# The gate softmax of a product-key layer moved out of its top-k, behind blocks of the expert product

## The chip, the cores and the metric

One core of one Trainium2 chip runs the whole program. The metric is device time in microseconds (us) of one execution; smaller is better. Engines are named as in the profile: PE is TensorE, ACT is ScalarE, DVE is VectorE, POOL is GpSimd, SP is SyncE, which issues most of the DMAs.

## The reference

A decoder block on 512 tokens of width 1024: a gated convolution and a differential attention, a layer norm, then a PEER channel mixer and another layer norm. The change lies in the mixer, which has 16,384 experts (rows of `u` and `v`), 8 heads and 16 chosen experts for each token and head:

```python
q = (xc @ wq).reshape(PEER_CHUNK, PEER_HEADS, 2, PEER_DHALF)
sc = jnp.einsum('chpd,hpnd->chpn', q, keys)
s1, i1 = lax.top_k(sc[:, :, 0], PEER_TOPK)
s2, i2 = lax.top_k(sc[:, :, 1], PEER_TOPK)
cand = (s1[..., :, None] + s2[..., None, :]).reshape(...)
top_s, pos = lax.top_k(cand, PEER_TOPK)
eidx = jnp.take_along_axis(cidx, pos, axis=-1)
g = jax.nn.softmax(top_s, axis=-1)
act = jax.nn.gelu(jnp.einsum('chkd,cd->chk', u[eidx], xc))
return jnp.einsum('chk,chkd->cd', g * act, v[eidx])
```

The softmax `g` over the 16 best scores of a token and head is what the change moves.

## The kernel before, in words

The tokens form four chunks of 128. For chunks 0 to 2 (384 tokens) the mixer is computed densely: for each of 128 blocks of 128 experts, `dense_u` (L426) forms u·x for all 384 tokens on TensorE (24 matmuls of 128x384, three per slice of the contraction, because float32 is split in a high and a low part) and applies Gelu on ScalarE (L432). A dense matrix of gates, zero for experts that a token has not chosen, is multiplied in later (L561), and `dense_v` forms the second product with `v`. Chunk 3 gathers its experts' rows by DMA (`gather_steps`, L495).

The weights of a block come by DMA; `split` (L71) makes the high part on ScalarE (`whi`, L72) and the low part (`wlo`, L73) on GpSimd for blocks 0 to 13 (`NPOOL`) and on VectorE from block 14 on. Two PSUM tiles (`psH`) take the products, so block j+2 can start only when block j's Gelu has read its tile. 42 blocks of u·x (`HS_BUFS`) precede the second product; from there the two products alternate until the end.

The gate matrix is made meanwhile. `topk` (L276) runs on VectorE for one chunk after the other: `top16` (L268) finds the 16 largest scores of each half and head by pairs of MAX8, FIND_INDEX8 and MATCH_REPLACE8, then those of the candidates `cand`; L299 to L304 make the softmax (subtract, Exp on ScalarE, sum, reciprocal, product `g`); L305 to L330 turn positions into the expert's two index halves `idf`. `topk_transpose` (L333) transposes `idf` and `g` on TensorE (L337, L338), and ScalarE and VectorE copy them out as `iT` and `gT` (L340 to L343). From those, the loop at L455 makes one-hot tiles `oa`, `bh` and `bl` for 16 tokens at a time on VectorE (L462 to L465), multiplies them on TensorE (L470, L471), copies the result out on ScalarE (`stg`, L472) and writes it to a buffer `G_D` in device memory (L473). There are 24 such steps. `dense_w` (L544) reads `G_D` back (`gt`, L553) before the second product starts, and loads rows of v (`vr`, L540).

Each engine executes its instructions in one fixed order, which a scheduler computes when the program is built, from its own model of the durations. The source steers it only by edges: `tc.issue_after(x)` keeps what is made inside it behind instruction x on the same engine. The table TK says behind which expert block each chunk's transposes are put; the code around it, before:

```python
    for c in range(NDC):
        for j in range(*TK[c]):
            mm = dense_u(j)
        with tc.issue_after(mm.ins):
            topk_transpose(c, *picked[c])
```

With `TK = ((0, 3), (3, 10), (10, 14))` chunk 0's transposes stand behind block 2, chunk 1's behind block 9, chunk 2's behind block 13.

Of the kernel before, what the change touches and what calls it, by code (L numbers as in the profile page):

```python
# [9 lines left out]
F32 = mybir.dt.float32  # L10
# [4 lines left out]
AF = mybir.ActivationFunctionType  # L15
ALU = mybir.AluOpType
AX = mybir.AxisListType
# [7 lines left out]
PH = 8  # L25
# [3 lines left out]
ND = 384  # L29
# [11 lines left out]
VR = 3  # L41
WB = 4
GA = 4
TK = ((0, 3), (3, 10), (10, 14))
GI2 = 8
GP = 3
GSCALE = 16384.0
# [6 lines left out]
def build(nc, tc, I, out, dbg=None):  # L54
# [155 lines left out]
    for h in range(NH):  # L210
        ps = proj(12 + h)
        nc.scalar.copy(out=qz[0:64, h, 0, :], in_=ps[0:64])
        nc.scalar.copy(out=qz[64:128, h, 1, :], in_=ps[64:128])
        ps = proj(16 + h)
        nc.scalar.copy(out=kT[:, h, :], in_=ps)
        ps = proj(20 + h)
# [42 lines left out]
    tk = tk_ctx.enter_context(load_pool("topk", bufs=1, side="left"))  # L259
# [16 lines left out]
    def topk(tk, sc, nb):  # L276
        m = tk.tile([128, 2, PH, 16], F32, name="m", bufs=nb)
        ix = tk.tile([128, 2, PH, 16], U32, name="ix")
        for h in range(PH):
# [10 lines left out]
            cand[:, :, 64:112].rearrange("p h (a b) -> p h a b", b=4),  # L290
            m[:, 0, :, 4:16].unsqueeze(3).broadcast_to([128, PH, 12, 4]),
            m[:, 1, :, 0:4].unsqueeze(2).broadcast_to([128, PH, 12, 4]), op=ALU.add)
        tsc = tk.tile([128, PH, 16], F32, name="tsc")
        pos = tk.tile([128, PH, 16], U32, name="pos")
        for h in range(PH):
            top16(tk, tsc[:, h, :], pos[:, h, :], cand[:, h, :], 112)
        g = tk.tile([128, 16, PH], F32, name="g", bufs=nb)
        gx = tk.tile([128, PH, 16], F32, name="gx")
        nc.vector.tensor_tensor(gx, tsc, tsc[:, :, 0:1].broadcast_to([128, PH, 16]), op=ALU.subtract)  # L299
        nc.scalar.activation(gx, gx, AF.Exp)  # L300
        gs = tk.tile([128, PH], F32, name="gs")
        nc.vector.tensor_reduce(gs, gx, axis=AX.X, op=ALU.add)
        nc.vector.reciprocal(gs, gs)
        nc.vector.tensor_tensor(g.rearrange("p k h -> p h k"), gx, gs.unsqueeze(2).broadcast_to([128, PH, 16]), op=ALU.mult)  # L304
        u1 = tk.tile([128, PH, 16], U32, name="u1")  # L305
        u2 = tk.tile([128, PH, 16], U32, name="u2")
        ab = tk.tile([128, 2, 16, PH], F16, name="ab")
# [10 lines left out]
        idf = tk.tile([128, 2, 128], F32, name="idf", bufs=nb)  # L318
# [9 lines left out]
        for n in (8, 4, 2):  # L328
            nc.vector.tensor_tensor(e[:, :, 0:n], e[:, :, 0:n], e[:, :, n:2 * n], op=ALU.add)  # L329
        nc.vector.tensor_tensor(idf, e[:, :, 0], e[:, :, 1], op=ALU.add)  # L330
        return idf, g

    def topk_transpose(c, idf, g):  # L333
        cs = slice(c * 128, (c + 1) * 128)
        tp = psG.tile([128, 4, 128], F32, name="psX", bufs=1)
        for p in range(2):
            nc.tensor.transpose(tp[:, p, :], idf[:, p], ident)  # L337
        nc.tensor.transpose(tp[:, 2, :], g.rearrange("p k h -> p (k h)"), ident)  # L338
        for e in range(2):
            nc.scalar.copy(out=iT[:, :, cs, e], in_=tp[:, 0:2, :])  # L340
            nc.scalar.activation(gT[:, 0, cs, e], tp[:, 2, :], AF.Copy, scale=GSCALE)
        for e in range(2):
            nc.vector.scalar_tensor_tensor(gT[:, 1, cs, e], tp[:, 2, :], GSCALE, gT[:, 0, cs, e],  # L343
                                           op0=ALU.mult, op1=ALU.subtract)
# [81 lines left out]
    def dense_u(j):  # L426
        uh, ul = wblock(I["uT"][j], nc.gpsimd if j < NPOOL else nc.vector)
        ps = psH.tile([128, S], F32, name="psH")
        for k in range(NK):
            mm = mm3(ps[:, 0:ND], uh[:, k, :], ul[:, k, :], x1h[:, k, 0:ND], x1l[:, k, 0:ND], k == 0, k == NK - 1)  # L430
        hs = hsp.tile([128, ND], F32, name="hs")
        nc.scalar.activation(hs, ps[:, 0:ND], AF.Gelu)  # L432
        hidden[j] = hs
        return mm

    picked = []
    for c in range(NDC):
# [3 lines left out]
        picked.append(topk(tk, scs[c], 2))  # L441
    for c in range(NDC):
        for j in range(*TK[c]):
            mm = dense_u(j)
        with tc.issue_after(mm.ins):
            topk_transpose(c, *picked[c])


# [6 lines left out]
    for tb in range(NTG):  # L455
# [10 lines left out]
        for o0 in range(0, TG, 4):  # L466
            ps = psG.tile([128, 4, 128], F32, name="psG")
# [26 lines left out]

    def gather_steps():  # L495
        with tc.issue_after(gate):
            idf, g = topk(t3, sc3, 1)
        for p in range(2):
            nc.vector.scalar_tensor_tensor(idx[:, p, :], idf[:, p], 128.0, idf[:, 1 - p], op0=ALU.mult, op1=ALU.add)
        nc.vector.tensor_copy(gw, g.rearrange("p k h -> p (k h)"))  # L500
# [151 lines left out]
```

## Time and profile before

| what | value |
|---|---|
| median of 3 runs | 1518.4 us |
| runs | 1518.4, 1519.96, 1514.06 us |
| the profiled execution, its own time | 1515.57 us |
| its span in the trace | 1513.8 us |
| mean granted clock of TensorE | 0.985 |
| busy: PE, DVE, ACT, POOL | 1452.1, 1183.8, 592.9, 476.7 us |

The span is the time from the first to the last instruction in the trace; the execution's own time lies 1.8 us above it. Busy time is an average over stages that have different limits, so a stage is to be looked at by itself. The stage that the change touches runs from about 330 us, when the top-k of chunk 0 ends, to about 630 us, when the second product starts.

### The profile page before, as it was taken

What the parts mean: (1) busy time and instruction counts of PE and PEld (TensorE: products, weight loads), DVE (VectorE), ACT (ScalarE), POOL (GpSimd) and SP (SyncE); (2) the same over time, 40 slices, a digit from 0 to 9 for tenths busy, and PEclk for the clock granted to TensorE, in tenths of its full rate; (3) what the DMA queues carried; (4) which work ended last, traced back from release to release, by engine and by line L of the source; (5) the groups of instructions that cost most, each with busy time, mean ns of one, the idle gap of its engine ahead of it and who ended that gap; (6) DMA issues with size and microseconds to landing.
All of it is one profiled execution on the core that took longest, in us unless ns stands there. A gap on an engine that the chain in (4) does not pass through costs nothing.

```text
span 1513.8 us, 22123 instructions
## 1 busy us (share of the span) xinstructions
PE 1452.1 (96%) x8097; PEld 1299.5 (86%) x8097; DVE 1183.8 (78%) x2373; ACT 592.9 (39%) x932; POOL 476.7 (31%) x322
## 2 busy tenths in 40 slices
PE   7999988997799999899999999999999999999996
PEld 5787867997798999888989999899899999998985
DVE  4546545579999887699888888888888888888745
ACT  3544244452345555334433333333333333333342
POOL 1000043674430000000345454445444544444200
PEclk9999999999899999999999999999999999999999
DMA  6111263454436666996799999999999999999731
GB/s 254 62 65 58 96 208 131 156 197 131 139 130 228 242 233 250 298 295 193 264 377 339 350 334 346 344 333 344 334 357 329 350 333 344 334 340 346 275 126 70
DMA packets 146429, 375.94 MB, mean 248 GB/s; under 512 B 16272, under 2 KB 63376, under 8 KB 142992
## 3 DMA queue, kind: packets, MB, share of 16 engines
q1 hardware_dynamic: 100960, 203.97, 39.8%
q0 software_dynamic: 36864, 134.23, 24.3%
q10 hardware_dynamic: 8496, 36.32, 6.3%
q8 instruction: 63, 1.03, 0.3%
q14 instruction: 46, 0.38, 0.1%
HBM read 343.55 MB, written 30.93 MB: 247 GB/s over the span
## 4 chain that ended last, share of the span: by engine, by line
PE 82%; DVE 12%; DMA 3%; ACT 1%; issue 1%; SPq 0%; POOL 0%; ACTq 0%; DVEq 0%; POOLq 0%
PE psH L86 14%; PE psH L84 14%; PE psH L85 14%; PE acc L84 11%; PE acc L85 11%; PE acc L86 11%; PE psG L470 1%; PE psS L180 1%; PE psG L471 1%; DVE rest L272 1%; DVE sc L325 1%; DMA raw<-w_out 1%; DVE sc L329 1%; DVE ix L274 1%; DVE ix L271 1%
## 5 line engine op out<-in xcount | busy, mean ns | idle before, releaser
L84 PE MATMUL psH<-x1Th,whi 128*128 128x384 f32 (+1 forms) x1280 | 423.7, 331 | 15.0 <-ACT hs L432 15.0
L86 PE MATMUL psH<-x1Th,wlo 128*128 128x384 f32 (+1 forms) x1280 | 423.0, 330 | 3.7 <-DVE wlo L73 2.5
L85 PE MATMUL psH<-x1Tl,whi 128*128 128x384 f32 (+1 forms) x1280 | 420.9, 329 | 0.0
L72 ACT CAST whi<-raw 128x1024 fp32r<-128x1024 f32 x200 | 209.7, 1050 | 435.9 <-PE psH L85 313.6
L508 POOL DMA_INDIRECT row<-u,idx x128 | 169.5, 1324 | 457.8 <-ACT hs L432 290.3
L85 PE MATMUL acc<-vl,wh 128*128 128x512 f32 x756 | 294.4, 389 | 0.0
L86 PE MATMUL acc<-vh,wl 128*128 128x512 f32 x756 | 294.3, 389 | 0.0
L84 PE MATMUL acc<-vh,wh 128*128 128x512 f32 x756 | 288.9, 391 | 4.4 <-ACT vh L72 4.4
L84 PEld LDWEIGHTS psH<-x1Th,whi 128*128 128x128 f32 x1280 | 243.9, 191 | 19.3 <-ACT hs L432 15.7
L73 DVE TENSOR_TENSOR wlo<-raw,whi 128x1024 fp32r<-128x1024 f32 x146 | 180.0, 1233 | 92.1 <-ACT whi L72 90.6
L86 PEld LDWEIGHTS psH<-x1Th,wlo 128*128 128x128 f32 x1280 | 243.9, 191 | 5.7 <-DVE wlo L73 3.4
L85 PEld LDWEIGHTS psH<-x1Tl,whi 128*128 128x128 f32 x1280 | 244.1, 191 | 3.2
L73 POOL TENSOR_TENSOR wlo<-raw,whi 128x1024 fp32r<-128x1024 f32 x54 | 136.0, 2522 | 300.7 <-ACT whi L72 299.8
L508 POOL DMA_INDIRECT row<-v,idx x128 | 166.1, 1298 | 183.7 <-DVE x L523 136.2
L72 ACT CAST wh<-hs 128x384 fp32r<-128x384 f32 x128 | 65.6, 514 | 322.1 <-PE acc L85 318.2
L84 PEld LDWEIGHTS acc<-vh,wh 128*128 128x128 f32 x756 | 142.2, 188 | 30.9 <-ACT vh L72 4.8
L86 PEld LDWEIGHTS acc<-vh,wl 128*128 128x128 f32 x756 | 142.0, 188 | 29.0
L73 DVE TENSOR_TENSOR vl<-vr,vh 128x1024 fp32r<-128x1024 f32 x126 | 154.3, 1224 | 16.0 <-ACT vh L72 15.7
L523 DVE SCALAR_TENSOR_TENSOR x<-row,gw,x 128x1024 f32<-128x1024 f32 x128 | 164.0, 1281 | 3.5 <-DMA row<-v,idx 2.6
L85 PEld LDWEIGHTS acc<-vl,wh 128*128 128x128 f32 x756 | 142.0, 188 | 26.0
L516 DVE SCALAR_TENSOR_TENSOR row<-row,x 128x1024 f32<-128x1024 f32 x128 | 154.7, 1221 | 10.7 <-DMA row<-u,idx 10.7
L72 ACT CAST vh<-vr 128x1024 fp32r<-128x1024 f32 x126 | 131.9, 1048 | 0.1
(196 smaller groups left out, 1668.5 us busy)
## 6 DMA issues: line engine op xcount, KB each, us to landing
raw<-uT SPq DMA_DIRECT2D x128, 512.0 KB, 5.4
vr<-v SPq DMA_DIRECT2D x128, 512.0 KB, 5.4
G_D<-stg ACTq DMA_DIRECT2D x24, 1024.0 KB, 4.7
gt<-G_D SPq DMA_DIRECT2D x46, 512.0 KB, 7.9
raw<-wq SPq DMA_DIRECT2D x32, 512.0 KB, 3.4
raw<-w_in SPq DMA_DIRECT2D x24, 512.0 KB, 3.4
raw<-w_out SPq DMA_DIRECT2D x16, 512.0 KB, 4.7
xr<-xT SPq DMA_DIRECT2D x4, 512.0 KB, 6.5
```

The lines of the kernel that those rows point to most:

```text
L72: nc.scalar.copy(out=hi, in_=raw)
L73: return sub.tensor_sub(lo, raw, hi.bitcast(F32))
L84: nc.tensor.matmul(ps, lh, rh, start=first, stop=False)
L85: nc.tensor.matmul(ps, lh, rl, start=False, stop=False)
L86: return nc.tensor.matmul(ps, ll, rh, start=False, stop=last)
L180: nc.tensor.matmul(sp[:, p, 0:w], qz[:, h, p, qs], kT[:, h, 0:w], start=True, stop=False)
L271: nc.vector.max_index(pos[:, 0:8], vals[:, 0:8], src)
L272: nc.vector.match_replace(t[:, 0:n], vals[:, 0:8], src, -3.0e38)
L274: nc.vector.max_index(pos[:, 8:16], vals[:, 8:16], t[:, 0:n])
L508: ins = nc.gpsimd.indirect_dma_start(out=t, out_offset=None, in_=I["uv"[p]], in_offset=bass.IndirectOffsetOnAxis(ap=idx[:, p, k:k + 1], ax ...
L516: nc.vector.scalar_tensor_tensor(t, t, 1.0, x1, op0=ALU.mult, op1=ALU.mult, accum_out=dots[:, k:k + 1])
L523: nc.vector.scalar_tensor_tensor(x1, t, gw[:, k:k + 1], x1, op0=ALU.mult, op1=ALU.add, accum_out=tots[:, GCH:GCH + 1] if k == 127 else None)
```

## The change

The softmax leaves `topk` and becomes a function `gates`. It is called at the head of `topk_transpose`, and in `gather_steps` right after `topk`. `topk` now returns the best scores `tsc`, which get a buffer for each chunk, in place of `g`. `dense_u` also returns its Gelu instruction, and `topk_transpose` stands under two edges: behind the last matmul of the stated block on TensorE, and behind its Gelu on ScalarE. The instructions on VectorE have no such edge. TK's first entry goes from block 2 to block 5; the other two stay.

```diff
--- before.py
+++ after.py
@@ -41,7 +41,7 @@
 VR = 3
 WB = 4
 GA = 4
-TK = ((0, 3), (3, 10), (10, 14))
+TK = ((0, 6), (6, 10), (10, 14))
 GI2 = 8
 GP = 3
 GSCALE = 16384.0
@@ -290,18 +290,10 @@
             cand[:, :, 64:112].rearrange("p h (a b) -> p h a b", b=4),
             m[:, 0, :, 4:16].unsqueeze(3).broadcast_to([128, PH, 12, 4]),
             m[:, 1, :, 0:4].unsqueeze(2).broadcast_to([128, PH, 12, 4]), op=ALU.add)
-        tsc = tk.tile([128, PH, 16], F32, name="tsc")
+        tsc = tk.tile([128, PH, 16], F32, name="tsc", bufs=nb)
         pos = tk.tile([128, PH, 16], U32, name="pos")
         for h in range(PH):
             top16(tk, tsc[:, h, :], pos[:, h, :], cand[:, h, :], 112)
-        g = tk.tile([128, 16, PH], F32, name="g", bufs=nb)
-        gx = tk.tile([128, PH, 16], F32, name="gx")
-        nc.vector.tensor_tensor(gx, tsc, tsc[:, :, 0:1].broadcast_to([128, PH, 16]), op=ALU.subtract)
-        nc.scalar.activation(gx, gx, AF.Exp)
-        gs = tk.tile([128, PH], F32, name="gs")
-        nc.vector.tensor_reduce(gs, gx, axis=AX.X, op=ALU.add)
-        nc.vector.reciprocal(gs, gs)
-        nc.vector.tensor_tensor(g.rearrange("p k h -> p h k"), gx, gs.unsqueeze(2).broadcast_to([128, PH, 16]), op=ALU.mult)
         u1 = tk.tile([128, PH, 16], U32, name="u1")
         u2 = tk.tile([128, PH, 16], U32, name="u2")
         ab = tk.tile([128, 2, 16, PH], F16, name="ab")
@@ -328,9 +320,21 @@
         for n in (8, 4, 2):
             nc.vector.tensor_tensor(e[:, :, 0:n], e[:, :, 0:n], e[:, :, n:2 * n], op=ALU.add)
         nc.vector.tensor_tensor(idf, e[:, :, 0], e[:, :, 1], op=ALU.add)
-        return idf, g
-
-    def topk_transpose(c, idf, g):
+        return idf, tsc
+
+    def gates(tk, tsc, nb):
+        g = tk.tile([128, 16, PH], F32, name="g", bufs=nb)
+        gx = tk.tile([128, PH, 16], F32, name="gx")
+        nc.vector.tensor_tensor(gx, tsc, tsc[:, :, 0:1].broadcast_to([128, PH, 16]), op=ALU.subtract)
+        nc.scalar.activation(gx, gx, AF.Exp)
+        gs = tk.tile([128, PH], F32, name="gs")
+        nc.vector.tensor_reduce(gs, gx, axis=AX.X, op=ALU.add)
+        nc.vector.reciprocal(gs, gs)
+        nc.vector.tensor_tensor(g.rearrange("p k h -> p h k"), gx, gs.unsqueeze(2).broadcast_to([128, PH, 16]), op=ALU.mult)
+        return g
+
+    def topk_transpose(c, idf, tsc):
+        g = gates(tk, tsc, 2)
         cs = slice(c * 128, (c + 1) * 128)
         tp = psG.tile([128, 4, 128], F32, name="psX", bufs=1)
         for p in range(2):
@@ -429,9 +433,9 @@
         for k in range(NK):
             mm = mm3(ps[:, 0:ND], uh[:, k, :], ul[:, k, :], x1h[:, k, 0:ND], x1l[:, k, 0:ND], k == 0, k == NK - 1)
         hs = hsp.tile([128, ND], F32, name="hs")
-        nc.scalar.activation(hs, ps[:, 0:ND], AF.Gelu)
+        act = nc.scalar.activation(hs, ps[:, 0:ND], AF.Gelu)
         hidden[j] = hs
-        return mm
+        return mm, act
 
     picked = []
     for c in range(NDC):
@@ -441,8 +445,8 @@
         picked.append(topk(tk, scs[c], 2))
     for c in range(NDC):
         for j in range(*TK[c]):
-            mm = dense_u(j)
-        with tc.issue_after(mm.ins):
+            mm, act = dense_u(j)
+        with tc.issue_after(mm.ins), tc.issue_after(act.ins):
             topk_transpose(c, *picked[c])
 
 
@@ -494,7 +498,8 @@
 
     def gather_steps():
         with tc.issue_after(gate):
-            idf, g = topk(t3, sc3, 1)
+            idf, tsc = topk(t3, sc3, 1)
+            g = gates(t3, tsc, 1)
         for p in range(2):
             nc.vector.scalar_tensor_tensor(idx[:, p, :], idf[:, p], 128.0, idf[:, 1 - p], op0=ALU.mult, op1=ALU.add)
         nc.vector.tensor_copy(gw, g.rearrange("p k h -> p (k h)"))
```

What the edges do to the engines' orders is seen best in the orders themselves. A number behind a name tells apart buffers of that name.

**ScalarE, around the first expert blocks.** `gx` is the softmax's input, of chunk 1 in the first piece and of chunk 0 in the second; `hs` is a Gelu's output, blocks 0 to 2 before, blocks 5 to 7 after. Before:

```order
L395 COPY qT_3117<-psH_3092 128x256
L300 ACTIVATE gx_3467<-gx_3467 128x128
L72 CAST whi_3745<-raw_3744 128x1024
L409 COPY scst_3120<-psT_3010 128x512
L409 COPY scst_3124<-psT_3011 128x512
L410 DMA SC_D0_70<-scst_3120 128x512
L410 DMA SC_D1_71<-scst_3124 128x512
L432 ACT_TABLE_LOAD
L432 ACTIVATE hs_3709<-psH_3684 128x384
L72 CAST whi_3788<-raw_3787 128x1024
L432 ACTIVATE hs_3742<-psH_3717 128x384
```

And now:

```order
L436 ACTIVATE hs_3850<-psH_3825 128x384
L329 ACT_TABLE_LOAD
L329 ACTIVATE gx_3853<-gx_3853 128x128
L72 CAST whi_3937<-raw_3936 128x1024
L436 ACT_TABLE_LOAD
L436 ACTIVATE hs_3901<-psH_3876 128x384
L344 CAST iT_1502<-psX_3860 128x2x128
L345 ACTIVATE gT_1503<-psX_3860 128x128
L344 CAST iT_1502<-psX_3860 128x2x128
L345 ACTIVATE gT_1503<-psX_3860 128x128
L72 CAST whi_3970<-raw_3969 128x1024
L436 ACTIVATE hs_3934<-psH_3909 128x384
```

Before, the Exp of chunk 1 stood ahead of the last score copies and of block 0's Gelu, and chunk 0's earlier still, among the scores. Now the Exp of chunk 0 follows the Gelu of block 5, with a table load on either side, and those of chunks 1 and 2 follow the Gelus of blocks 9 and 13 in the same way; the score copies are followed at once by block 0's Gelu.

**TensorE, at chunk 0's transposes.** `psX` is their tile; `psH` tiles are expert blocks, 2 and 3 before (3750, 3793). Before:

```order
L85 MATMUL psH_3750<-x1Tl_1497,whi_3745 128x384
L86 MATMUL psH_3750<-x1Th_1496,wlo_3746 128x384
L337 MATMUL psX_3777<-ident_101,idf_3305 128x128 x2
L338 MATMUL psX_3777<-ident_101,g_3285 128x128
L84 MATMUL psH_3793<-x1Th_1496,whi_3788 128x384
L85 MATMUL psH_3793<-x1Tl_1497,whi_3788 128x384
```

And now, at the change from block 6 (3876) to block 7 (3909):

```order
L85 MATMUL psH_3876<-x1Tl_1497,whi_3871 128x384
L86 MATMUL psH_3876<-x1Th_1496,wlo_3872 128x384
L84 MATMUL psH_3909<-x1Th_1496,whi_3904 128x384
L85 MATMUL psH_3909<-x1Tl_1497,whi_3904 128x384
L342 MATMUL psX_3860<-ident_101,g_3852 128x128
L86 MATMUL psH_3909<-x1Th_1496,wlo_3905 128x384
L84 MATMUL psH_3909<-x1Th_1496,whi_3904 128x384
```

The transpose of `g` moved from behind block 2 to two matmuls into block 7; those of `idf` now stand behind block 5.

**VectorE, at chunk 0's sum, reciprocal and product.** `rest` is a tile of a top-16, of chunk 1 in the first piece (m_3314) and of chunk 2 in the second (m_3481). Before:

```order
L303 RECIPROCAL gs_3289<-gs_3289 128x8
L274 MAX_INDEX ix_3315<-m_3314,rest_3322 128x8
L272 MATCH_REPLACE rest_3328<-m_3314,sc_1726 128x128
L325 TENSOR_TENSOR sc_1725<-sc_1725,ixf_3231 128x2048
L321 TENSOR_TENSOR sc_1725<-ab_3295,iota16_1507 128x2048
L304 TENSOR_TENSOR g_3285<-gx_3286,gs_3289 128x8x16
L272 MATCH_REPLACE rest_3334<-m_3314,sc_1726 128x128
L273 MAX m_3314<-rest_3328 128x8
L325 TENSOR_TENSOR sc_1725<-sc_1725,ixf_3231 128x2048
```

And now:

```order
L273 MAX m_3481<-rest_3549 128x8
L274 MAX_INDEX ix_3482<-m_3481,rest_3543 128x8
L331 TENSOR_REDUCE gs_3856<-gx_3853 128x8
L274 MAX_INDEX ix_3482<-m_3481,rest_3549 128x8
L272 MATCH_REPLACE rest_3555<-m_3481,sc_3479 128x128
L332 RECIPROCAL gs_3856<-gs_3856 128x8
L272 MATCH_REPLACE rest_3561<-m_3481,sc_3479 128x128
L273 MAX m_3481<-rest_3555 128x8
L333 TENSOR_TENSOR g_3852<-gx_3853,gs_3856 128x8x16
L273 MAX m_3481<-rest_3561 128x8
L274 MAX_INDEX ix_3482<-m_3481,rest_3555 128x8
L328 TENSOR_TENSOR gx_4003<-tsc_3408 128x128
```

Before, the three stood within chunk 0's own index building and the first top-16 of chunk 1. Now all of chunk 1's top-k, ending in its `idf`, stands ahead of them, and then 67 top-16 instructions of chunk 2: 28 MAX, 27 MAX_INDEX and 12 MATCH_REPLACE ahead of the sum, and four more ahead of the product. The first one-hot (L466) stands behind the last top-16 of chunk 2's scores.

**ScalarE, at the end of the one-hots.** `stg` is the copy of a one-hot product, the DMA to `G_D_69` writes it out, `hs` is a Gelu of the later blocks. Before:

```order
L472 ACTIVATE stg_5302<-psG_5330 128x128x4
L472 ACTIVATE stg_5302<-psG_5340 128x128x4
L72 CAST whi_6335<-raw_6334 128x1024
L432 ACTIVATE hs_6262<-psH_6237 128x384
L473 DMA G_D_69<-stg_5302 128x2048
L72 CAST whi_6399<-raw_6398 128x1024
L432 ACTIVATE hs_6295<-psH_6270 128x384
L72 CAST whi_6463<-raw_6462 128x1024
```

And now:

```order
L72 CAST whi_6335<-raw_6334 128x1024
L436 ACTIVATE hs_6262<-psH_6237 128x384
L476 ACTIVATE stg_5302<-psG_5310 128x128x4
L476 ACTIVATE stg_5302<-psG_5320 128x128x4
L476 ACTIVATE stg_5302<-psG_5330 128x128x4
L72 CAST whi_6399<-raw_6398 128x1024
L436 ACTIVATE hs_6295<-psH_6270 128x384
L476 ACTIVATE stg_5302<-psG_5340 128x128x4
L477 DMA G_D_69<-stg_5302 128x2048
L72 CAST whi_6463<-raw_6462 128x1024
```

The last copy moved behind one more weight cast and Gelu. On TensorE the blocks behind the last one-hot product and ahead of the second product's first matmul went from 74 matmuls to 47. On SyncE one more weight load (`raw`, 512 KB) stands ahead of the first loads of `gt`.

## Rows read from the trace of the kernel before

**Rows 1.** The page, part 1: busy us, share of the span, instructions by engine
```profile
PE 1452.1 (96%) x8097; PEld 1299.5 (86%) x8097; DVE 1183.8 (78%) x2373; ACT 592.9 (39%) x932; POOL 476.7 (31%) x322
```

**Rows 2.** Busy us of each engine by stretch, then PEclk, DMA share, GB/s
```profile
350.00:400.00 50.00, 35.00 (x218) 34.58 (x217) 49.90 (x206) 15.44 (x26) 21.05 (x9) 0.83 0.37 128
400.00:450.00 50.00, 45.24 (x303) 43.39 (x301) 50.00 (x177) 22.25 (x36) 21.49 (x8) 0.97 0.35 116
...
900.00:1100.00 200.00, 200.00 (x998) 180.44 (x997) 171.47 (x282) 71.51 (x99) 97.30 (x74) 1.00 0.95 342
```

**Rows 3.** Waits of PE from 355 to 470 us: total, times, longest
```profile
PE psH L84 <- ACT hs L432: 15.0, 1, 15.0
PE psG L470 <- DVE bh L464: 4.2, 1, 4.2
PE psH L86 <- DVE wlo L73: 2.5, 2, 1.5
```

**Rows 4.** Timeline of ACT, 358 to 450 us: start, us, instruction, idle before
```profile
378.69 0.31 ACT L300 ACTIVATE gx<-gx 128x128 f32<-128x128 f32 x1 [17.15 <-DVE gx L299]
...
382.67 1.28 ACT L432 ACT_TABLE_LOAD   x1 [1.77 <-DMA SC_D<-scst]
...
400.09 1.05 ACT L72 CAST whi<-raw 128x1024 fp32r<-128x1024 f32 x1 [2.72 <-POOL wlo L73]
...
404.25 1.05 ACT L72 CAST whi<-raw 128x1024 fp32r<-128x1024 f32 x1 [2.72 <-POOL wlo L73]
...
445.26 1.28 ACT L432 ACT_TABLE_LOAD   x1
446.55 0.49 ACT L432 ACTIVATE hs<-psH 128x384 f32<-128x384 f32 x1
```

**Rows 5.** Chain of waits, 330 to 465 us: start, us, what
```profile
336.38 0.27 DVE gs L302
...
345.12 2.40 DVE g L304
...
363.25 0.39 DVE m L273 x2
363.63 0.52 DVE ix L274 x2
...
391.94 0.42 DVE idf L330
...
449.44 0.38 DVE g L304
449.81 1.05 DVE wlo L73
...
456.13 1.14 DVE wlo L73
```

**Rows 6.** Busy us by stretch behind two waits, for PEclk
```profile
385.00:390.00 5.00, 5.00 (x17) 5.00 (x17) 5.00 (x5) 0.78 (x2) 2.82 (x1) 0.50 0.80 317
...
625.00:630.00 5.00, 3.94 (x14) 3.44 (x15) 5.00 (x18) 2.72 (x5) 0.00 (x0) 0.66 1.14 335
```

**Rows 7.** Timeline of PE in three places
```profile
384.51 0.69 PE L84 MATMUL psH<-x1Th,whi 128*128 128x384 f32 x1 [15.00 <-ACT hs L432]
...
448.66 0.22 PE L471 MATMUL psG<-bl,oa 128*128 128x128 f16 x1
448.72 0.22 PE L470 MATMUL psG<-bh,oa 128*128 128x128 f16 x1
...
626.06 1.65 PE L84 MATMUL acc<-vh,wh 128*128 128x512 f32 x3 [4.44 <-ACT vh L72]
```

**Rows 8.** Chain of waits at the change of phase, 590 to 640 us
```profile
609.44 4.82 DMA G_D<-stg
...
618.98 4.74 DMA vr<-v
```

**Rows 9.** Timeline of POOL, 355 to 450 us
```profile
380.01 3.28 POOL L73 TENSOR_TENSOR wlo<-raw,whi 128x1024 fp32r<-128x1024 f32 x1 [16.27 <-ACT whi L72]
```

## The prediction

> **What bounds the kernel now.** I read the page first, then busy time by stretch, TensorE's waits, ScalarE's timeline, the chain of waits, and the two places where the diff moves work. All times are of the profiled execution: 1515.57 us, span 1513.8, the 1.8 us around the span unchanged. It lies 2.8 us below the median of the three runs (1518.4), so a change in its time is added to that median. A difference under 0.5% (7.6 us) is what a measurement of this kernel can't tell from none: faster means below 1510.8, slower above 1526.0.
>
> On the page TensorE is busy for 96% of the span [rows 1], and from 900 to 1100 us for all of it [rows 2]. Only stretches with gaps can give anything back. In 350–400 TensorE has 35.00 of 50 us busy and in 400–450 45.24, while VectorE has 49.90 and 50.00 [rows 2]. Both engines look guilty; the waits say how they hang together. TensorE's longest wait is 15.0 us at the first matmul of expert block 2, for block 0's Gelu; 4.2 us go to the first one-hot, 2.5 to two weight splits [rows 3]. ScalarE's timeline says why the Gelu was late: the Exp of chunk 1's gate softmax stood ahead of it, and ScalarE had idled 17.15 us for VectorE's subtraction behind that chunk's top-16 [rows 4]. Then come the score copies, a wait for their DMA and a table load. So the 15.0 us are a queue that stood in the wrong order, which the change rearranges.
>
> But the chain that ends the stage doesn't run through this wait. From 330 us on it is VectorE's in nearly every piece, through top-16 operations, index building and one-hots, up to the first two weight splits that VectorE makes for TensorE itself, block 14's at 449.81 and block 15's at 456.13 [rows 5]. Blocks 0 to 13 get their split from GpSimd, so TensorE can run ahead of VectorE until block 14, and there it waits (1.5 us, the longest of the two that make 2.5) [rows 3]. **TensorE's 15 us are slack against that split**: had it run through them, it would have stood the longer at block 14.
>
> **The change, step by step.**
>
> *1. Exp leaves ScalarE's early queue.* Removed: the 17.15 us wait and with it TensorE's 15.0 at block 2, and what followed: 5 us at granted clock 0.50, the 1.2 GHz level [rows 6], about 2.6 us of work lost with the half microsecond ahead of them. Block 2 will still wait some 2.5 us, since block 0's Gelu stays behind the last score copies, a DMA wait (1.77) and a table load [rows 4]. Behind that, VectorE stays full; nothing of the 15.0 reaches the end by itself.
>
> *2. What TensorE does then.* Blocks 2 to 6 run at the pitch of 4.16 us that blocks 4 to 5 show (400.09 to 404.25, [rows 4]), from the stop of block 1 at 384.51 - 15.00 = 369.5 [rows 7] plus those 2.5 us: 372 + 5 x 4.16 = 393, or up to 397 if the casts come late. Then come two matmuls of block 7 and the transpose of g of chunk 0, which the order now puts there. When is that g ready? In VectorE's new order its sum, reciprocal and product stand behind all of chunk 1's top-k and 67 operations of chunk 2's top-16: 28 maxima at 0.19, 27 index searches at 0.26 [rows 5] and 12 replacements that take as long as those, 28 x 0.19 + 39 x 0.26 = 15.5 us, and about 1.9 for four more such operations, the sum, the reciprocal and the product (0.38, [rows 5]). Chunk 1's idf ended at 391.94 + 0.42 = 392.4 [rows 5]. Ahead of it the early gates of chunk 0 fall away (sum 0.27, the reciprocal, which I count alike, and the product that took 2.40 at 345.12, [rows 5]), and chunk 1's subtraction, sum and product with them, about half a microsecond: 3.4 us in all. So idf of chunk 1 comes at 389.0 and g at 389.0 + 17.4 = 406. **TensorE waits there some 9 to 13 us in place of the 15.0**, all for VectorE, and then again some 2 to 4 us for the first one-hot, as now. The clock falls again as after the old wait, so its 2.6 us return as well. Until then GpSimd and ScalarE idle as they did before, a few microseconds later.
>
> *3. The end of the VectorE chain.* From idf of chunk 1 to block 14's split VectorE took 449.81 - 392.4 = 57.4 us. In the new order the same 120 top-16 operations stand in that stretch; the gates of chunks 0 and 1 (2 x 0.9 us: sum 0.27, reciprocal alike, product 0.38), a subtraction (0.2) and two index operations of a microsecond each come in, two one-hot products (as long) and the gates of chunk 2 (0.9) go out: about +1.0. So the split starts at 389.0 + 57.4 + 1.0 = 447.4, 2.4 earlier. Between this split and the next stand two operations in the new order, some 1.8 us, where 456.13 - 450.9 = 5.3 us lay before [rows 5], so TensorE's second wait (2.5 - 1.5 = 1.0) goes. Against this, TensorE has done 7 one-hot groups by then, not 10; three groups of eight matmuls, 448.72 - 448.66 = 0.06 us apart [rows 7], are 1.4 us still to do, 1.7 with the change-overs between the kinds. **Gain here 2.4 + 1.0 - 1.7 = 1.7 us.** From below: the whole early saving might be lost to collisions (rival 2), -2; from above +5.
>
> *4. The switch to the second phase.* At 609 us the last one-hot's copy is written out, its DMA takes 4.82 us, the gate tiles are loaded, then the first expert rows (4.74) [rows 8], and TensorE starts the second product at 626.06 after 4.44 us idle [rows 7]. The DMAs are covered by blocks of the first product that are queued behind the last one-hot: 74 matmuls before, 47 now. The work ahead of the second product's first matmul is the same, but 27 x 0.173 (4.16/24) = 4.7 us of it now stand ahead of the last one-hot. The chain of DMAs starts 4.7 later, less the 1.7 of step 3: **the second product starts 3.0 us later**, and its wait grows from 4.4 to about 9.1. A longer wait costs clock: after the 4.44 us the granted clock was 0.66 over 3.94 us of busy time, a loss of 0.34 x 3.94 = 1.3 us; after the 15.0 it was 0.50 for 5 us, a loss of 2.6 with what lay ahead [rows 6]. Between no extra and the difference of 1.3 I take 0.9. On SyncE one 512 KB weight load now stands ahead of the gate loads; its buffer is free before they may start, so it costs nothing unless it delays them (at most about 1.5, kept for the range). On ScalarE the last copy of the one-hots moves behind a weight cast and a Gelu (1.05 and 0.49, [rows 4]), which is within the 4.7 already counted, as it waits for TensorE anyway.
>
> *5. Table loads.* Two per Exp among the Gelus, three more in all. The row shows 1.28 us and the Gelu starting right behind (445.26 + 1.28, 446.55) [rows 4]: 3.8 us on an engine that is 39% busy [rows 1], each beside a TensorE that has two blocks' buffers and 4.16 us per block. Nothing in the sum; if the cover were gone, 3.8 at most. The Trainium skill, "ScalarE: Activation LUTs", section "What ACT_TABLE_LOAD costs", speaks against such a change: it adds a drain of about 1.38 us to each switch, so 2.66 in all. The trace disagrees, with 0.01 us between load and Gelu; by the page the three would be 8.0 us, still beside other work.
>
> Sum: -1.7 (step 3) + 4.7 + 0.9 (step 4) = **+3.9 us**: own time 1519.5, and on the median 1518.4 + 3.9 = **1522**. Ends from the unknowns: -5 + 4.7 = about 1518 and +2 + 4.7 + 1.3 + 1.5 = about 1528.
>
> **Rivals.**
>
> *Rival 1, the wait is really gone (faster).* If VectorE reaches g of chunk 0 before TensorE reaches block 7, and the split of block 14 comes earlier by as much, then up to 15.0 + 2.6 us come back: 1500.8; half of it would be 1510. For it: the wait was ScalarE's, not VectorE's, and the clock loss behind it was real. Against it: VectorE has 49.90 and 50.00 of 50 us busy on either side [rows 2], and the order puts g behind 67 operations. It needs VectorE to shed about 8 us, which only fewer collisions with GpSimd could give. Chance 0.11.
>
> *Rival 2, VectorE is slowed by GpSimd (slower).* The same product g took 2.40 us at 345.12 and 0.38 at 449.44 [rows 5]. The first ran while GpSimd made splits, the second after the last of them; the split at 380.01 took 3.28 us [rows 9]. So a VectorE operation that reads two tiles can be held up 2.0 us by a split. Before, GpSimd was idle for 16.27 us ahead of 380.01 [rows 9], and two splits fell on the building of chunk 1's index up to 392.4, that one and the next. With ScalarE free, blocks 2 to 6 are split at 4.16 us there: in those 13 us three or four. The one-hots later see two fewer, so I count nothing. But where four more meet two-tile operations the chain ends 8 us later: 1530. It decides the sign from two more collisions on (1522 + 4.0 = 1526). The Trainium skill, "SBUF — State Buffer", section "SBUF: two separate sides", has the rule: VectorE with two SBUF inputs and GpSimd share a port pair as an exclusive lock, held for a whole instruction. The 2.40 against 0.38 agrees. Chance 0.17.
>
> *Rival 3, nothing is lost at the switch.* If TensorE's lead at block 14 is 5 us, or the loads come sooner than with the queue before, step 4 is paid: 1518.4. Against it: the 27 matmuls are in the order. That the edges do not bind, and the softmax stays where it was, is excluded: the order shows it moved. Chance 0.10, inside "same".
>
> **How the numbers follow.** Forecast 0.62 (its own range 1518 to 1528; the part above 1526 is worth 0.02), rival 3 0.10, rival 1 0.11, rival 2 0.17. Range: 1511 to 1531, which leaves out most of rival 1 and the tail of rival 2. Faster 0.11, slower 0.17 + 0.02 = 0.19, same 0.62 - 0.02 + 0.10 = 0.70.
>
> **What would show it.** Right: no wait at block 2 over 4 us, but one of 9 to 15 at the transpose of g, for VectorE's product; VectorE full from 355 to 445; block 14's split within 3 us of 447; the wait at the second product near 9. Wrong: no long wait of TensorE before block 14, or a split of block 14 at 440 or before (rival 1), or after 453 (rival 2); a wait at the switch under 5 (rival 3).

## The result and the profile after

The changed kernel takes 1525.42 us in the median of 11 runs (1520.83 to 1530.54), the kernel before 1516.35 in as many (1510.64 to 1519.96). The ratio is 1.0062, with a 95% interval of 1.0045 to 1.0079: slower, by some 9 us. The profiled execution has a span of 1523.0 us against 1513.8. Timed once more in another set of runs, the changed kernel had a median of 1523.23 and a ratio of 1.0051 (1.0033 to 1.0069).

The engines' busy time, in the page's first part, hardly moved from [rows 1]:

```profile
PE 1448.9 (95%) x8097; PEld 1296.7 (85%) x8097; DVE 1186.6 (78%) x2373; ACT 597.4 (39%) x935; POOL 465.7 (31%) x322
```

TensorE has 3 us less, VectorE 3 and ScalarE 4.5 more. The stretches say where the time went (columns as in [rows 2]):

```profile
350.00:400.00 50.00, 39.52 (x253) 38.84 (x251) 49.80 (x177) 20.18 (x28) 28.05 (x11) 0.96 0.52 169
400.00:450.00 50.00, 35.46 (x228) 34.08 (x228) 49.97 (x201) 19.23 (x33) 13.17 (x5) 0.83 0.21 74
```

From 350 to 400 TensorE is now busy for 39.52 us where it had 35.00, so the old wait is gone from there. From 400 to 450 it has 35.46 against 45.24: the gap has moved and grown. VectorE is full in both as before. TensorE's waits from 355 to 650 us give names to the gaps:

```profile
PE psX L342 <- DVE g L333: 21.3, 1, 21.3
PE acc L84 <- ACT vh L72: 9.3, 1, 9.3
PE psH L86 <- DVE wlo L73: 3.9, 1, 3.9
PE psH L84 <- ACT hs L436: 1.9, 1, 1.9
```

The 15.0 us at block 2 of [rows 3] have become 1.9; in their place stands one wait of 21.3 us at the transpose of chunk 0's g, for VectorE's product. The wait for block 14's split is 3.9 (1.5 before), that at the second product 9.3 (4.44 in [rows 7]). The chain of waits, to be held against [rows 5]:

```profile
356.22 0.32 DVE idf L322
...
364.43 2.77 DVE sc L285
...
376.22 1.44 DVE u L301
...
378.83 1.14 DVE sc L313
379.97 2.87 DVE ab L309
...
383.89 3.35 DVE sc L313
...
388.53 3.31 DVE sc L321
...
392.59 2.46 DVE sc L321
395.07 0.42 DVE idf L322
...
412.31 0.28 DVE g L333
...
450.80 1.15 DVE wlo L73
451.99 0.69 PE psH L86
```

Chunk 0's index ends at 356.54 us, 4.5 earlier than before, since its gates are out of the way. Chunk 1's ends at 395.49, 3.1 us *later*. Between the two lie 38.95 us, against 31.33 before (361.03 to 392.36). Four operations in the last part of this stretch are two us too long: 2.87, 3.35, 3.31 and 2.46. Undisturbed ones of these kinds took 0.64, 1.14, 1.06 and 0.43 in the two traces, so the excess is 2.2 + 2.2 + 2.3 + 2.0 = 8.7 us. Before, two were hit there (2.78 and 3.20 us, together 4.3 too long). A fifth, at 364.43, is 2.2 us over the 0.59 that it took before, and a sixth, `u` at 376.22, 1.2 over the 0.2 us of its kind; a split ran beside each of these two as well (364.26 to 366.66, 375.18 to 377.57). GpSimd's timeline shows what ran beside the four:

```profile
379.34 2.90 POOL L73 TENSOR_TENSOR wlo<-raw,whi 128x1024 fp32r<-128x1024 f32 x1 [1.77 <-ACT whi L72]
383.50 2.66 POOL L73 TENSOR_TENSOR wlo<-raw,whi 128x1024 fp32r<-128x1024 f32 x1 [1.26 <-ACT whi L72]
387.66 3.09 POOL L73 TENSOR_TENSOR wlo<-raw,whi 128x1024 fp32r<-128x1024 f32 x1 [1.51 <-ACT whi L72]
392.06 2.69 POOL L73 TENSOR_TENSOR wlo<-raw,whi 128x1024 fp32r<-128x1024 f32 x1 [1.32 <-ACT whi L72]
419.75 2.40 POOL L73 TENSOR_TENSOR wlo<-raw,whi 128x1024 fp32r<-128x1024 f32 x1 [25.00 <-ACT whi L72]
```

One split for each of them, at the pitch of the expert blocks, where [rows 9] had a pause of 16.27 us up to 380.01. The new pause, of 25.00 us, lies behind 394, beside top-16 operations. Those are not held up by a split: beside the one at 370.67 they took their usual 0.16 to 0.26 us.

The row at 451.99 in the chain is the second surprise: the first matmul behind block 14's wait takes 0.69 us. The stretches there, and the change of phase:

```profile
451.99:455.00 3.01, 3.01 (x9) 3.01 (x10) 3.01 (x5) 0.00 (x0) 0.00 (x0) 0.50 0.58 177
455.00:460.00 5.00, 5.00 (x29) 4.84 (x29) 3.02 (x7) 1.40 (x2) 0.00 (x0) 0.72 0.34 108
```

```profile
618.48 4.81 DMA G_D<-stg
...
623.88 7.02 DMA gt<-G_D
...
634.80 1.65 PE acc L84 x3
```

From 451.99 to 455 TensorE was granted 0.50, the 1.2 GHz level, and over the next 5 us 0.72; its loss is 3.01 x 0.50 + 5.00 x 0.28 = 2.9 us. Behind the 1.5 us wait of the kernel before it had the full clock. At the change of phase the last copy's DMA starts at 618.48 instead of 609.44 ([rows 8]) and the second product at 634.80 instead of 626.06: 8.7 of the span's 9.2 us are there by then.

The table loads are as forecast:

```profile
367.88 1.28 ACT L436 ACT_TABLE_LOAD   x1 [2.73 <-DMA SC_D<-scst]
369.17 0.49 ACT L436 ACTIVATE hs<-psH 128x384 f32<-128x384 f32 x1
```

One takes 1.28 us, and the Gelu follows after 0.01.

### The profile page after: what moved, and what is told of

It reads as the page before. It is cut to its first block, busy times and chain, and to the rows that moved or that the text cites. A ratio compares the mean times of both kernels' runs of the same rounds, so it can differ in the third digit from the quotient of the medians.

```text
span 1523.0 us, 22128 instructions
## 1 busy us (share of the span) xinstructions
PE 1448.9 (95%) x8097; PEld 1296.7 (85%) x8097; DVE 1186.6 (78%) x2373; ACT 597.4 (39%) x935; POOL 465.7 (31%) x322
## 4 chain that ended last, share of the span: by engine, by line
PE 83%; DVE 12%; DMA 3%; ACT 1%; issue 0%; POOL 0%; SPq 0%; ACTq 0%; DVEq 0%
PE psH L86 14%; PE psH L84 14%; PE psH L85 14%; PE acc L84 11%; PE acc L86 11%; PE acc L85 11%; PE psG L474 1%; PE psG L475 1%; PE psS L180 1%; DVE rest L272 1%; DVE sc L321 1%; DVE sc L313 1%; DMA raw<-w_in 1%; DVE sc L317 1%; DVE ix L274 1%; DVE ix L271 1%
## 5 line engine op out<-in xcount | busy, mean ns | idle before, releaser
L513 POOL DMA_INDIRECT row<-u,idx x128 | 162.4, 1269 | 475.6 <-ACT whi L72 301.1
```

The lines of the kernel that those rows point to most:

```text
L513: ins = nc.gpsimd.indirect_dma_start(out=t, out_offset=None, in_=I["uv"[p]], in_offset=bass.IndirectOffsetOnAxis(ap=idx[:, p, k:k + 1], ax ...
```

## The experiments

Theory A, formed from the two traces: the loss has two parts. Some 4.7 us are expert matmuls that the new order puts ahead of the last one-hot, so that they no longer cover the DMAs at the change of phase. The rest arises ahead of 460 us, where GpSimd's splits, no longer held back by ScalarE, hit VectorE's index building and bring block 14's split late. The rivals: B, the table loads and Exps among the Gelus cost the time; C, the wait for g costs its own length; D, the index is late for another reason than the splits.

**The table alone.** The kernel before with the table's first entry at block 6.

```diff
-TK = ((0, 3), (3, 10), (10, 14))
+TK = ((0, 6), (6, 10), (10, 14))
```

> The kernel before with the table's first entry at block 6 alone: the softmax stays in the top-k and the Exps keep their early places on ScalarE. Theory A (the 9 us have two parts: some 4.7 us because fewer expert matmuls stand behind the last one-hot, and some 4.5 us because GpSimd, no longer held up by ScalarE, makes its splits while VectorE builds chunk 1's index, so that block 14's split, the 3.9 us wait for it and the slow clock behind that come late): TensorE keeps its 15 us at block 2, GpSimd its 16 us pause, index of chunk 1 done within 2 us of 392, block 14's split near 450; 66 matmuls behind the last one-hot against 74 cost 1.4, so 1516 to 1519. Rival B (the three more table loads and the Exps among the Gelus cost the time, on ScalarE): none of them here, 1516. Rival C (the place of the transposes costs it, whatever the softmax does): 1522 or more.

1518.54 us, ratio 1.0013 (1.0001 to 1.0025). The order of this kernel is, instruction by instruction, that of the changed kernel without the edge on ScalarE: taking the softmax out of the top-k moves nothing by itself, the edge does. Its chain:

```profile
363.50 0.33 DVE idf L330
...
394.74 0.43 DVE idf L330
...
453.04 1.15 DVE wlo L73
```

The profiled execution had chunk 0's index 2.8 us later than the kernel before, so that chunk 1's (395.2) and the split (453.0) miss the expected times by as much; from index to index it took 31.34 us, as before. Theory A's time holds; B's 1516 is only just outside the interval, C's 1522 is far out. From the last one-hot to the second product this kernel took 19.3 us, against 17.6 in the kernel before, and waited 7.6 there.

**The edge alone.** The changed kernel with the old table, that is the edge on ScalarE without the later block.

```diff
-TK = ((0, 6), (6, 10), (10, 14))
+TK = ((0, 3), (3, 10), (10, 14))
```

> The changed kernel with the old table entry, block 3: the softmax outside the top-k and held behind the Gelu of block 2. Theory A: GpSimd runs on from 370 as in the changed kernel, chunk 1's index is done at 394 to 397 and block 14's split at 450 to 452; 47 matmuls behind the last one-hot, so a wait of 9 us at the second product; 1522 to 1527. Rival B: as many table loads, the same. Rival C (the wait for chunk 0's g, 21.3 us, costs the time by its length): g now stands behind 40 top-16 operations instead of 71, some 8 us earlier, so the wait is near 15 and the time 1518 to 1521.

1520.05 us, ratio 1.0031 (1.0019 to 1.0043), below theory A's range. Its waits:

```profile
PE psX L342 <- DVE g L333: 14.4, 2, 10.9
PE acc L84 <- ACT vh L72: 9.3, 1, 9.3
...
PE psH L86 <- DVE wlo L73: 0.6, 1, 0.6
```

The wait at the second product is 9.3 us as foreseen, but the index of chunk 1 came at 390.59 (33.38 us behind chunk 0's), and block 14's split at 447.39. Theory A was wrong that the splits cost this kernel as much as the changed one. Of the two parts, this kernel has the one at the change of phase. That g stands 31 operations earlier and the time is 5 us lower is what C said too, so this run doesn't tell C from a shorter index.

**More cover behind the last one-hot.** The last n blocks ahead of the second product are held behind the last one-hot's matmul; n = 3 on the changed kernel, 4 on the kernel before.

```diff
-                nc.tensor.matmul(ps[:, t, :], oa[:, q, :], bl[:, q, :], start=False, stop=True)
+                oh = nc.tensor.matmul(ps[:, t, :], oa[:, q, :], bl[:, q, :], start=False, stop=True)
...
-    while nu < HS_BUFS:
+    while nu < HS_BUFS - n:
         dense_u(nu)
         nu += 1
+    with tc.issue_after(oh.ins):
+        while nu < HS_BUFS:
+            dense_u(nu)
+            nu += 1
```

> The changed kernel with the last three expert blocks ahead of the second product held behind the last one-hot's matmul, so that 113 matmuls stand there instead of 47; the order ahead of that is the same. Theory A: the last one-hot comes 66 x 0.173 = 11.4 us earlier, if VectorE has its tiles ready, the 9.3 us wait at the second product goes and with it most of the slow clock behind it: 1513 to 1518. If the one-hot tiles are late instead: waits for VectorE near 590 us in place of the 9.3. Rival B and rival C: the loss lies ahead of 470 us, so the second product starts later all the same and the time stays within 3 us of 1525.

> The kernel before with its last four expert blocks ahead of the second product held behind the last one-hot's matmul: 113 matmuls there instead of 74. Theory A: the wait of 4.4 us at the second product and the slow clock behind it (1.3 us) go, 1510 to 1512. If the wait is worth nothing there, because the path goes through something else: 1516.

On the changed kernel 1515.36 us, ratio 0.9995 (0.9984 to 1.0005): the whole loss is gone, although the table loads and the order up to the last one-hots are the same and TensorE still waits 17.4 us for g. B and C as causes of the whole loss fall with this. A part of it they could still be, covered by a gain at the change of phase; against that stands the kernel before with the same 113 matmuls, without the new table loads and the wait for g and not faster, and for C the early softmax below. On the kernel before 1517.41, ratio 1.0002 (0.9992 to 1.0012): nothing gained, where theory A said 4 to 6 us. Their waits behind 475 us, first the changed kernel's:

```profile
PE psG L474 <- DVE bh L468: 2.2, 1, 2.2
PE psG L475 <- DVE bl L469: 0.8, 1, 0.8
PE psG L474 <- ACT stg L476: 0.6, 1, 0.6
PE psH L86 <- DVE wlo L73: 0.6, 1, 0.6
```

```profile
PE psG L471 <- DVE bl L465: 3.1, 1, 3.1
PE psH L86 <- DVE wlo L73: 1.8, 1, 1.8
PE psG L470 <- ACT stg L472: 0.9, 2, 0.7
```

Neither waits for vh at the second product any more, but TensorE now waits for one-hot tiles and late splits, 4.2 and 5.8 us, and from the last one-hot to the second product it takes 21.5 and 23.4 us instead of 17.6. And the second product starts with work left over: in these two orders 7 and 31 matmuls of the first product stand behind its first matmul that stood ahead of it, at 0.173 us each 1.2 and 5.4 us. So the kernel before was near a balance: pulling its one-hots forward exchanges one wait for another.

**The cover that the change took away, and no more.** As above, n = 1: 72 matmuls against 74 in the kernel before. Run twice.

> The changed kernel with one expert block held behind the last one-hot's matmul: 72 matmuls stand there, against 47 in the changed kernel, 74 in the kernel before and 113 in the run with three blocks held. Theory A (at the switch each matmul that is missing behind the last one-hot costs its 0.173 us until the wait is gone): wait at the second product 9.3 - 25 x 0.173 = 5.0 us, the slow clock behind it as short as before, so 1525.4 - 4.3 - 0.9 = 1520, and block 14's split at 448 to 451 as in the changed kernel. Rival (what the run with three held blocks gave back came from somewhere else, since TensorE waited for one-hot tiles there instead): 1514 to 1517 or 1524 and more, and a wait that does not follow the count.

> The run with 72 matmuls behind the last one-hot once more: its profile (split of block 14 at 444.11, span 1513.4) was the fastest of its executions, 8 us under their median of 1523.24. Theory A: the median is near 1521 (1525.4 and 1523.2 for the changed kernel, less 4.3 of cover, plus about 1 for a longer chain of DMAs), and the time from block 14's split to the second product is again 181 us, where the changed kernel has 184. Rival (held blocks give nothing until the wait is gone): 1523 to 1526, and 183 us or more.

1523.24 us (ratio 1.0048, 1.0031 to 1.0065) and 1519.71 (1.0022, 1.0012 to 1.0031). Theory A's 1520 and 1521 lie between the two; the first is a miss, the second fits. The profile says why less comes back than the count promises:

```profile
608.55 8.81 DMA G_D<-stg
...
619.66 7.31 DMA vr<-v
...
628.50 1.65 PE acc L84 x3
```

In the second run the write of the last one-hot took 8.81 us and the first expert rows 7.31, where [rows 8] has 4.82 and 4.74, and the wait was 8.2 instead of 5.0. From the last one-hot to the second product lay 20.0 us in the first profile and 21.0 in the second, against 17.6 to 17.7 in the kernel before and the changed one. The number of matmuls held there does not fix this time, for the table alone (66) took 19.3 and the run with the splits held back, below (51), 19.9. From block 14's split to the second product it took 181.1 and 183.5 us, against 184.0 in the changed kernel: one profile for theory A, one for the rival. Of the 2.4 us between the two, 1.0 is the chain of DMAs and 1.5 the clock behind the wait at block 14: over the next 10 us TensorE was granted 0.85 in the first and 0.70 in the second.

**The splits held back.** GpSimd's split of block 2 waits for chunk 1's index.

```diff
-        split(raw, hi, lo, sub)
+        ins = split(raw, hi, lo, sub)
+        if hold[0] is not None:
+            tc.add_manual_dep(ins.ins, hold[0].name, PACED, reason="GpSimd's splits wait for the index")
...
+            hold[0] = idf_ins[1] if j == 2 else None
             mm, act = dense_u(j)
+            hold[0] = None
```

> The changed kernel with GpSimd's split of block 2, and by its order those behind it, waiting until VectorE has finished chunk 1's index. Theory A (each split that falls on the index building holds one two-tile operation of VectorE for some 2.2 us, four of them in the changed kernel's 379 to 395 us): no operation of that stretch over 1.5 us, chunk 1's index 28 to 30 us behind chunk 0's instead of 38.95, so at 385 to 388; TensorE waits some 17 us at block 2 instead of 21 at g; block 14's split at 443 to 448 instead of 450.8; 51 matmuls behind the last one-hot, wait 8 to 9 there; 1517 to 1521. Rival D (the index is late for another reason, such as operations put ahead of it by the order): index at 393 or later, 1524 and more.

1523.23 us, ratio 1.0052 (1.0035 to 1.0070): the time is a miss. The mechanism is not. The indices of chunks 0 and 1:

```profile
356.85 0.32 DVE idf L327
...
383.72 0.44 DVE idf L327
```

Without splits beside it the stretch from index to index is 27.0 us, and no single operation of it is over 1.5. With the excesses added it gives the other two: 27.0 + 4.3 = 31.3 for the kernel before (31.33), 27.0 + 8.7 + 2.2 + 1.2 = 39.1 for the changed one (38.95). D falls. Block 14's split came at 446.03. But it was not what TensorE waited for:

```profile
PE psH L90 <- POOL wlo L73: 14.4, 1, 14.4
PE acc L88 <- ACT vh L72: 10.7, 1, 10.7
PE psX L347 <- DVE g L338: 4.5, 1, 4.5
```

With 14.4 us lost at block 2 and 4.5 at g, TensorE was behind VectorE at block 14 (it did not wait for that split), and its 51 matmuls behind the last one-hot left a wait of 10.7. So this kernel shows the price of the splits, and also that TensorE's waiting is slack only as long as block 14's split is still the later of the two.

**The softmax of chunk 0 earlier.** The gates of chunk 0 are put behind block 0's Gelu instead of block 5's, the transposes stay.

```diff
+EX = (0, 9, 13)
...
             mm, act = dense_u(j)
+            for e in range(NDC):
+                if j == EX[e]:
+                    with tc.issue_after(act.ins):
+                        picked[e] = picked[e][0], gates(tk, picked[e][1], 2)
```

> The changed kernel with its table, but the softmax of chunk 0 held behind the Gelu of block 0 instead of block 5, and with its own edge ahead of the transposes: g of chunk 0 then stands next to chunk 1's index on VectorE, ahead of all of chunk 2's top-16, and 58 matmuls stand behind the last one-hot. Theory A (the wait for g is slack against block 14's split): the wait for g falls below 8 us, block 14's split comes within 2 us of 447 to 449 and the time is that of the old table less 11 x 0.173 = 1.9: 1516 to 1520. Rival C (the wait for g costs its length): 10 us below the old table's 1520, 1508 to 1511.

1517.12 us, ratio 1.0016 (1.0003 to 1.0029).

```profile
PE psG L478 <- DVE bh L472: 9.9, 1, 9.9
PE acc L85 <- ACT wh L73: 6.6, 1, 6.6
PE psX L342 <- DVE g L334: 5.8, 1, 5.8
```

The wait for g fell to 5.8 us, and 9.9 appeared at the first one-hot, for the same engine; block 14's split was at 448.42. Theory A's numbers hold. C's 1508 to 1511 is out: taking 15 us from the wait for g left the split within the 445.3 to 450.8 that the changed kernel itself shows (below) and a new wait behind.

**The changed kernel again.**

> The changed kernel once more, unchanged. Theory A (which VectorE operations a split meets hangs on microseconds, so the stretch from chunk 0's index to chunk 1's differs between executions of one and the same order): 33 to 39 us against 38.95 in the first profile, and the span moves with block 14's split: 1523 less what that split is ahead of 450.8. Rival D (the order alone fixes it, and the two runs with other orders behind the one-hots were shorter for a reason of their own): 38.5 to 39.4 us and a span of 1521 to 1524. The median stays 1523 to 1527 by both.

1523.23 us. The profiled execution was the quickest of six, 1518.77 us with a span of 1517.0:

```profile
354.56 0.32 DVE idf L322
...
389.99 0.42 DVE idf L322
...
445.27 1.15 DVE wlo L73
```

From index to index 35.53 us, not 38.95, and block 14's split at 445.27, 5.5 us ahead of the first profile; the span is 6.0 shorter. One order, two executions: D is out here as well. What did not move is the way from block 14's split to the second product: 183.7 us (628.93 - 445.27) after 184.0, against 176.2 in the kernel before (626.06 - 449.81). So some 7.5 us are the part of the loss that both profiles share, and the split's time is the part that varies. Over the five profiles with this order (the changed kernel's two, n = 3, and n = 1 twice) the stretch was 38.95, 35.53, 35.59, 33.36 and 33.41 us. With the old order on ScalarE (the kernel before, the table alone, n = 4) it was 31.33, 31.34 and 31.35.

**Looking for a version ahead of both.** The old table with n = 3, and the early softmax with n = 1 and 2.

> The run with the old table entry and its 47 matmuls behind the last one-hot, with three blocks held behind it: 113. Theory A: the wait of 9.3 us at the second product goes, some 3 to 4 us of waits for one-hot tiles come near 590 us, as in the other two runs with 113; 1520.05 - 6 = 1511 to 1515, ahead of both kernels. Rival (VectorE's one-hots set the end of the phase whatever stands behind them, as the kernel before with 113 showed): 1515 to 1518.

> The run with the softmax of chunk 0 behind block 0's Gelu, with one expert block held behind the last one-hot: 72 matmuls there instead of 58. By the count alone 14 x 0.173 = 2.4 us are gained, 1514 to 1515; if the chain of DMAs grows as in the other run with 72 (20 us from the last one-hot to the second product against 17), nothing is: 1516 to 1518.

> The same with two blocks held: 96 matmuls behind the last one-hot. If the chain of DMAs stays at 20 to 21 us, the wait at the second product is gone, 1511 to 1514; if one-hot tiles come late near 590 us by as much as the wait shrinks, 1515 to 1517.

1514.74 us (ratio 1.0000, 0.9986 to 1.0014), 1516.82 (1.0006, 0.9992 to 1.0019) and 1517.44 (1.0003, 0.9989 to 1.0017). All three are ahead of the changed kernel and none is ahead of the kernel before. The first time is within theory A's range, but its "ahead of both" is a miss; with the table loads of the changed kernel it is not behind the kernel before, with 74 matmuls or with 113, so no cost of B shows there. The second came out on its no-gain side, though its chain from the last one-hot to the second product was 18.0 us in the profile, not 20 (16.9 with 58 matmuls). The third is just past its upper range, and not for late one-hot tiles: the chain took 22.0 us, with a write of 9.80, and TensorE still waited 5.1 us at the second product.

## Why the prediction was right or wrong

The forecast was 1522, a loss of 3.9 us that a measurement could not tell from none; the time came out at 1525.4, inside the range, and the loss at 9, clear of no change. Slower had 0.19. That the time lies as near as 3.4 us is partly luck: the base of 1518.4, a median of three runs, was 2.1 above the 1516.35 of eleven, so the loss is out by 5. Of the signs that were to show the forecast right, the waits at block 2 and at the second product and the full VectorE came; the wait for g (21.3 for 9 to 15) and block 14's split (450.8 for 447 ± 3) did not in the first profile.

*Steps 1 and 2, the wait moves to g*: right in kind, too short. The wait at block 2 came to 1.9 us (2.5 foreseen). TensorE reached g at 412.65 - 21.27 = 391.4 (393 to 397 foreseen), and g came at 412.6, not 406. All of the 6 us and more are in "idf of chunk 1 comes at 389.0": it came at 395.5. From there to g it was 17.1 us, with 17.4 foreseen.

*Step 3, the end of VectorE's chain*: the term that was mis-sized. Block 14's split was to start at 447.4, 2.4 us early; it started at 450.80, 1.0 late. I had seen one or two more splits fall on the index building and taken them as paid back later ("The one-hots later see two fewer, so I count nothing"). The index paid 7.6 us more (38.95 - 31.33); from there to the split VectorE took 55.3 instead of 57.45, 2.1 back, or 3.1 against my +1.0. This is rival 2's mechanism with its price of 2 us for each meeting, shown by the held-back splits; I gave it 0.17. The second profile of the same kernel had the split at 445.27, so the forecast lay between two executions. That its span, 1517.0 - 1513.8 = 3.2 us longer for a forecast of 3.9, fits is luck: the split was 2.1 us earlier than foreseen and the way from it to the second product 2 us longer (7.4 more than before, where steps 3 and 4 give 4.7 + 1.7 - 1.0 = 5.4), and it was the quickest of six executions.

A second miss in step 3: I let TensorE's second wait go (it did, 1.0) and kept the first at 1.5. It was 3.9 in every profile of this order, and the low clock behind it cost 2.9 us (1.5 to 3.0 in the five profiles) that no step had.

*Step 4, the change of phase*: right. The wait was to be 9.1 and was 9.3; the clock's extra was to be 0.9 and was some 0.4 (0.63 granted over the 5.20 us behind the wait, a loss of 1.9, against 0.62 over 3.94, 1.5). From block 14's split to the last one-hot TensorE took 166.3 us against 158.7 (617.08 - 450.80, 608.51 - 449.81), 7.6 more: 4.7 for the 27 matmuls, 1.7 for the one-hot groups still owed and 2.9 of clock, less the 1.0 of the vanished wait, make 8.3, 0.7 too many. The last one-hot is then 1.0 + 7.6 = 8.6 us later, and the second product 8.7. What the count of matmuls does not say is that buying the cover back pays less than 0.173 us each where the chain of DMAs takes longer, as it did in most runs with held blocks; why it does was not tested.

*Step 5, the table loads*: right; ScalarE's loads are the same in the runs that lost nothing (1515.36 and 1514.74).

*Rival 1* did not come: 15.0 us of waiting left TensorE's path at block 2 and came back at the next thing that VectorE owed. *Rival 3* did not either.

What stays open: the medians of kernels with one early order differ by more than their profiles explain. With 72 matmuls the two medians were 1523.24 and 1519.71, with 113 it was 1515.36; from block 14's split to the second product the last is only 1.3 to 3.7 us ahead of the others (179.8 against 181.1 and 183.5), 1.2 of it from the 7 matmuls that stand behind that point. How often an execution meets the costly alignment of splits and index operations can't be read from single profiles.

## What to carry to other kernels

A long wait of one engine is worth removing only if that engine is also the later one at the next point where it meets another; look which of the two is later there (here block 14's split). An instruction that holds back another engine may be shielding a third: GpSimd's pause, a by-product of the badly placed Exp, kept some of its splits off VectorE's index building. And where a stage ends in a chain of DMAs, count what is queued behind the instruction that starts the chain: a scheduler that moves 27 matmuls ahead of it can move the end by as much.

## What the runs showed of the hardware that was not expected

A GpSimd split of 2.4 us cost the two-tile VectorE operation that it met early 2.0 to 2.3 us whatever that operation's own length (0.43 to 1.14), while the top-16 operations beside it kept their 0.16 to 0.26. The held operation ends its own length behind the split: the split at 379.34 ends at 382.24 and `ab` 0.60 us later (own length 0.64), the one at 383.50 ends at 386.16 and `sc` 1.08 later (1.14). The Trainium skill, "SBUF — State Buffer", section "SBUF: two separate sides", says of such a pair that the one which starts first holds the shared ports for its whole instruction; the 2.0 to 2.3 of 2.4 us agree. In this case two tiles are not needed: the held `u` at 376.22 reads only one. Where GpSimd paused, three executions agreed to 0.02 us on a stretch of 31.3 us; where it ran, five differed by 5.6.

Behind the wait of 3.9 us at block 14 TensorE's granted clock fell to the 1.2 GHz level, and so it did behind the wait of 4.2 us for the first one-hot in the kernel before; behind the 1.5 us there it stayed at 1.00. The 10 us behind that wait for the one-hot:

```profile
413.01:423.01 10.00, 10.00 (x59) 9.68 (x59) 10.00 (x51) 1.92 (x3) 2.40 (x1) 0.83 0.15 53
```

That is a loss of 1.7 us. Behind five waits of one and the same length, 3.9 us, the same stretch had 0.71, 0.74, 0.85, 0.70 and 0.73, losses of 1.5 to 3.0: the length of a wait did not fix its price.
